# Weight loads of a two-layer encoder trunk: issued by Pool instead of SP

## The chip, the cores and the metric

One core of one Trainium2 chip. The core has five engines with queues of their own: TensorE (PE), VectorE (DVE), ScalarE (ACT), GpSimd (POOL) and SyncE (SP), and 16 DMA engines that they share. The metric is the device time of one execution in microseconds.

## The reference

Two encoder layers on 1024 tokens of width 1024, all in float32. In each layer

```
h = x * (1 + scale1(c)) + shift1(c)
x = LayerNorm(alpha * x + (1 + gate1(c)) * mix(h @ w_in) @ w_out)
h = x * (1 + scale2(c)) + shift2(c)
x = LayerNorm(alpha * x + (1 + gate2(c)) * (silu(h @ w_g) * (h @ w_u)) @ w_down)
```

`mix` is three groups of attention heads (A: differential, B: dilated windows, C: a local window with shared keys) side by side; `w_in` holds the queries, keys and values of all three. `w_g` and `w_u` stand side by side in `w_gu` (1024 x 5632, so 22 tiles of 128 columns each), `w_down` is 2816 x 1024. `scale`, `shift` and `gate` come from `silu(c) @ w_ada`.

## The kernel before

Activations lie transposed: a tile has 128 features on the partitions and tokens along the row. Every float32 product is made of three matmuls in a reduced format: each operand is split into a high part (ACT, a cast, line 162) and a low part (DVE, a subtraction, line 163), and high x high, high x low and low x high are summed (lines 302, 304, 306).

**Weights.** `load_w` (line 279) brings a column of 128 weights: for every four blocks of 128 rows one DMA (line 286) into a tile `raw` of 128 x 512 (256 KB, in runs of 512 bytes; 128 KB where only two blocks are left), which is then split into `wh` and `wl`. There are three `raw` buffers, two of `wh` and two of `wl`, so a load can start as soon as the split of the third load before it is done, and a split when PE has finished with the weights two columns back. `load_w` serves `w_in`, `w_out`, the first four tiles of the gate and `w_down`; for the very last group of `w_down` the split goes into 16 buffers `HW`, and all 8 columns are kept, as they are used twice.

**The gate.** Tiles 0 to 3 go through `gate` (line 1070) in two halves of the tokens with 32 loads by `load_w` in a layer. At the same time POOL makes the second half of the layer norm (lines 350, 372, 400) and the sums of the activations (`sums_h`, lines 1098 and 1101). The other 18 tiles go through `gate_all` (line 1111), a scheme with seven instead of eight block products: two DMAs of 512 KB (line 1120) fetch both columns into `E` (three buffers), POOL makes four sums of blocks `S1` to `S4` (line 1136), which are split into `WG` (10 buffers), PE makes the seven products (lines 1156 to 1158), POOL the last product with the silu (line 1195), and a DMA stores it (line 1196).

**Order.** Instructions are put in order on each engine by the framework's scheduler, which simulates a timeline; only some stretches of PE are kept in the order in which they are written. Each engine then works through its own row in order, and an instruction that waits holds up all that stand behind it on that engine. In the kernel before all DMAs are issued by SP: 1186 of them, of which the lines 286 and 1120 make 348 and 72. The rest are loads of `w_ada` (line 250), stores and fetches of attention's tiles (lines 570, 734 and others), of the hidden tiles (lines 1196, 1272) and of the output. POOL issues none; it rescales attention's probabilities (lines 597, 599, 881, 1019), and makes the parts of norm and gate named above.

Of the kernel before, what the change touches and what calls it, by code (L numbers as in the profile page):

```python
# [21 lines left out]
P = 128  # L22
NCH = 8
FH = 2816
# [80 lines left out]
class Trunk:  # L105
# [173 lines left out]
    def load_w(self, src, kt, parts=None):  # L279

        nc = self.nc
        wh, wl = parts or (self.t("wh", dt=F32R), self.t("wl", dt=F32R))
        for k in range(0, kt, 4):
            n = min(4, kt - k)
            raw = self.t("raw", (P, 512))
            nc.sync.dma_start(raw[:, :n * P].rearrange("p (k m) -> p k m", m=P), src[k * P:(k + n) * P].rearrange("(k p) m -> p k m", p=P))
            with self.tc.high_priority():
                self.split(wh[:, k * P:(k + n) * P], wl[:, k * P:(k + n) * P], raw[:, :n * P])
        return [a[:, :kt * P].rearrange("p (k m) -> p k m", m=P) for a in (wh, wl)]
# [120 lines left out]
    def first(self, X, H, side):  # L410
# [62 lines left out]

        columns(0, mods(0))
        wn = load_w(0)
        out = [self.t(tag, (P, 512)) for tag in ("S", "S", "S", "S", "MM", "MM")]
        for k in range(NCH):
            if k + 1 < NCH:
                acc = mods(k + 1)
            raw = wn  # L480
            if k + 1 < NCH:
                wn = load_w(k + 1)
            if k in self.X1:
                n = 4 // len(self.X1)
                for i in range(n):
                    load(4 + n * self.X1.index(k) + i)
            prepare(0, k)
            wh, wl = self.t("wh", dt=F32R), self.t("wl", dt=F32R)
            self.split(wh[:, :768], wl[:, :768], raw)
            ah, al = parts(H[k], 0)  # L490
            for c in range(6):
                w = slice(c * P, c * P + P)
                nc.tensor.matmul(out[c], wh[:, w], ah, start=k == 0, stop=False)
                nc.tensor.matmul(out[c], wh[:, w], al, start=False, stop=False)
                nc.tensor.matmul(out[c], wl[:, w], ah, start=False, stop=k == NCH - 1)
            if k + 1 < NCH:
                columns(k + 1, acc)
            for i in self.H1.get(k, ()):
                prepare(1, i)
            next(side, None)  # L500
# [610 lines left out]
    def gate_all(self, l, f, H, TS, hidden, last, side):  # L1111


        nc = self.nc
        q = [slice(256 * i, 256 * i + 256) for i in range(4)]
        raw = []
        for part in range(2):
            r = self.t("E")
            raw.append(r)
            nc.sync.dma_start(r.rearrange("p (k m) -> p k m", m=P), self.w_gu[l][:, part * FH + f * P:part * FH + (f + 1) * P].rearrange("(k p) m -> p k m", p=P))  # L1120
        a11, a12, a21, a22 = (raw[i // 2][:, 512 * (i % 2):512 * (i % 2) + 512] for i in range(4))
        ah, al = self.t("wh", dt=F32R), self.t("wl", dt=F32R)
        W = {}

        def ops(name, src):
            hi, lo = self.t("WG", (P, 512), F32R), self.t("WG", (P, 512), F32R)
            self.split(hi, lo, src)
            W[name] = (hi, lo)

        with self.tc.high_priority():  # L1130
            self.split(ah, al, raw[0])
            W["A11"], W["A12"] = ((ah[:, x], al[:, x]) for x in (slice(0, 512), slice(512, 1024)))
            s = {}
            for name, x, y, op in (("S1", a21, a22, ALU.add), ("S2", "S1", a11, ALU.subtract), ("S3", a11, a21, ALU.subtract), ("S4", a12, "S2", ALU.subtract)):
                s[name] = self.t("raw", (P, 512))
                nc.gpsimd.tensor_tensor(out=s[name], in0=s.get(x, x) if isinstance(x, str) else x, in1=s.get(y, y) if isinstance(y, str) else y, op=op)
                ops(name, s[name])
            ops("A22", a22)

        def quarter(name, half, j):  # L1140
            if name[0] == "T":
                c = q[int(name[1]) - 1]
                return [x[:, c] for x in TS[half, j]]
            k = 4 * (name[1] == "2") + j
            c = slice(256, 512) if name[2] == "1" else slice(0, 256)
            return [x[:, c] for x in H[k][half]]

        def product(tag, w, t):
            ps = self.t(tag, (P, 512))
            wh, wl = W[w]  # L1150
            for half in range(2):
                o = ps[:, 256 * half:256 * half + 256]
                for j in range(4):
                    c = slice(j * P, j * P + P)
                    th, tl = quarter(t, half, j)
                    nc.tensor.matmul(o, wh[:, c], th, start=j == 0, stop=False)  # L1156
                    nc.tensor.matmul(o, wh[:, c], tl, start=False, stop=False)  # L1157
                    nc.tensor.matmul(o, wl[:, c], th, start=False, stop=j == 3)  # L1158
            return ps

        prods = dict(P1=("MM", "A11", "B11"), P2=("MM", "A12", "B21"), P3=("TA", "S4", "B22"), P4=("S", "A22", "T4"),
                     P5=("S", "S1", "T1"), P6=("S", "S2", "T2"), P7=("S", "S3", "T3"))
        out = hidden[f].rearrange("p (h s c) -> p h s c", h=2, s=2)
        t = {}
        p = {}
        tt = lambda o, a, b, op: nc.vector.tensor_tensor(out=o, in0=a, in1=b, op=op)  # L1166
        new = lambda tag: self.t(tag, (P, 512))

        def step(n):
            p[n] = product(*prods[n])  # L1170
            next(side, None)

        def after1():
            t["a"] = new("ST")
            nc.scalar.copy(t["a"], p["P1"])

        def after6():
            t["b"] = new("ST")
            tt(t["b"], p["P6"], t["a"], ALU.add)

        def after7():
            t["c"] = new("TG")
            tt(t["c"], p["P7"], t["b"], ALU.add)

        def after5():
            t["d"] = new("TG")
            tt(t["d"], p["P5"], t["c"], ALU.add)
            tt(t["b"], p["P5"], t["b"], ALU.add)

        def after4():  # L1190
            tt(t["c"], t["c"], p["P4"], ALU.subtract)

        def finish(g, u, side):
            nc.scalar.activation(g, g, AF.Silu)  # L1194
            nc.gpsimd.tensor_tensor(out=u, in0=u, in1=g, op=ALU.mult)  # L1195
            nc.sync.dma_start(out[:, :, side], u.rearrange("p (h c) -> p h c", h=2))

        if last:
            for n in ("P6", "P7", "P5", "P4", "P1"):
                step(n)  # L1200
            after1(), after6(), after7(), after5(), after4()
        else:
            step("P1"), after1(), step("P6"), after6(), step("P7"), after7(), step("P5"), after5(), step("P4"), after4()
        step("P2")
        tt(t["a"], p["P2"], t["a"], ALU.add)
        finish(t["a"], t["c"], 1)
        step("P3")
        tt(t["b"], p["P3"], t["b"], ALU.add)
        finish(t["b"], t["d"], 0)
# [267 lines left out]
```

## Time and profile before

| | us |
|---|---|
| median of 3 runs | 2752.64 (2747.83 to 2754.9) |
| profiled execution | 2749.68 |
| its span, first to last instruction | 2747.8 |
| PE busy | 2603.6 (95%) |
| DVE busy | 1789.1 (65%) |
| ACT busy | 1122.0 (41%) |
| POOL busy | 866.7 (32%) |
| DMA engines, mean share | 40.0%, 332.90 MB, one queue of hardware |

The mean granted clock of TensorE was 0.982. The busy time of an engine counts neither its waits nor its issues of DMAs; SP's issues show as rows of `SPq` in the views of lines and queues. The stages of layer 1 lie, in us from the start of the span: norm and attention from 1398, `w_out` about 1930 to 2017, the first four tiles of the gate 2017 to 2125, `gate_all` 2125 to 2456, the down projection to 2683 and the last of it with the output to 2748. Layer 0 has the same stages from 50, 575, 664, 770 and 1130 on.

### The profile page before, as it was taken

To read this page: it belongs to the slowest core of one execution; us is meant where nothing else is said; L and a number is where in the kernel's file an instruction comes from. 1 tells how busy PE (TensorE), PEld (TensorE's weight loads), DVE (VectorE), ACT (ScalarE), POOL (GpSimd) and SP (SyncE) were. 2 spreads that over 40 slices of the span, in tenths; PEclk is the share of its full clock that TensorE was granted. 3 is DMA by queue.
4 is the path that set the end of the run, shared out by engine and by line. 5 is a ranking of instruction groups with operands and counts; after the bars stand their busy time and mean duration, and the time that the engine had idled before them with its cause. 6 is when DMAs were issued, how large, how long until landed. Compare 5 with 4: busy or idle time off the path is not lost.

```text
span 2747.8 us, 43777 instructions
## 1 busy us (share of the span) xinstructions
PE 2603.6 (95%) x16327; PEld 2217.1 (81%) x16327; DVE 1789.1 (65%) x3321; ACT 1122.0 (41%) x2255; POOL 866.7 (32%) x849
## 2 busy tenths in 40 slices
PE   6899988889999999999988999999999999999997
PEld 5788765668789999988867887766777999998887
DVE  7588746657867877745585887366487555545457
ACT  3466545523532222312244666466254323222124
POOL 4132322424634444200141323224256444430000
PEclk9999999999999999999999999999999999999999
DMA  8723342253454554643227223320425222236223
GB/s 270 223 79 92 128 125 75 56 184 89 158 157 146 169 154 143 195 161 105 74 88 236 81 77 119 107 57 10 138 89 180 89 77 86 78 100 215 81 81 115
DMA packets 389652, 335.69 MB, mean 122 GB/s; under 512 B 35096, under 2 KB 332096, under 8 KB 389440
## 3 DMA queue, kind: packets, MB, share of 16 engines
q1 hardware_dynamic: 389440, 332.90, 40.0%
q8 instruction: 129, 2.11, 0.3%
q14 instruction: 83, 0.68, 0.1%
HBM read 265.52 MB, written 67.31 MB: 121 GB/s over the span
## 4 chain that ended last, share of the span: by engine, by line
PE 60%; DMA 8%; DVE 7%; POOL 4%; issue 3%; ACT 2%; SPq 0%; DVEq 0%; POOLq 0%; ACTq 0%
PE S L306 5%; PE S L302 5%; PE S L304 5%; PE MM L306 4%; PE MM L302 4%; PE MM L304 4%; PE S L1156 4%; PE S L1157 4%; PE S L1158 4%; DMA MR<-in_w_ada 3%; PE MM L1158 2%; PE MM L1156 2%; PE MM L1157 2%; PE S L967 2%; PE MM L1042 1%
## 5 line engine op out<-in xcount | busy, mean ns | idle before, releaser
L162 ACT CAST wh<-raw 128x512 fp32r<-128x512 f32 x332 | 191.4, 603 | 518.1 <-PE S L304 224.7
L1156 PE MATMUL S<-O,WG 128*128 128x256 f32 x1152 | 325.1, 282 | 0.0
L1158 PE MATMUL S<-O,WG 128*128 128x256 f32 x1152 | 324.6, 282 | 0.0
L1157 PE MATMUL S<-O,WG 128*128 128x256 f32 x1152 | 324.4, 282 | 0.0
L163 DVE TENSOR_TENSOR wl<-raw,wh 128x512 fp32r<-128x512 f32 x332 | 259.7, 804 | 75.1 <-ACT wh L162 71.0
L306 PE MATMUL MM<-H,wl 128*128 128x512 f32 x624 | 248.9, 399 | 5.3 <-DVE wl L163 5.2
L302 PE MATMUL MM<-H,wh 128*128 128x512 f32 x624 | 247.8, 397 | 2.2 <-ACT wh L162 1.8
L304 PE MATMUL MM<-H,wh 128*128 128x512 f32 x624 | 249.0, 399 | 0.0
L1156 PEld LDWEIGHTS S<-O,WG 128*128 128x128 f32 x1152 | 217.1, 188 | 0.0
L1158 PEld LDWEIGHTS S<-O,WG 128*128 128x128 f32 x1152 | 217.0, 188 | 0.0
L1157 PEld LDWEIGHTS S<-O,WG 128*128 128x128 f32 x1152 | 217.0, 188 | 0.0
L162 ACT CAST WG<-raw 128x512 fp32r<-128x512 f32 x144 | 88.9, 621 | 289.0 <-PE S L1157 207.5
L1054 DVE SCALAR_TENSOR_TENSOR X<-S,der,X 128x512 f32<-128x512 f32 (+1 forms) x136 | 97.2, 718 | 162.4 <-PE S L306 150.8
L302 PE MATMUL S<-O,wh 128*128 128x512 f32 x496 | 193.4, 390 | 0.6 <-DVE der L274 0.6
L304 PE MATMUL S<-O,wh 128*128 128x512 f32 x496 | 193.0, 389 | 0.0
L306 PE MATMUL S<-O,wl 128*128 128x512 f32 x496 | 192.4, 391 | 0.5 <-DVE wl L163 0.5
L597 POOL TENSOR_SCALAR EX<-EX,Acf 128x384 f32<-128x384 f32 x64 | 70.2, 1098 | 386.8 <-DVE Acf L596 165.1
L1156 PE MATMUL MM<-H,wh 128*128 128x256 f32 x576 | 161.7, 281 | 1.1 <-DVE ST L1166 1.1
L1158 PE MATMUL MM<-H,wl 128*128 128x256 f32 x576 | 161.1, 280 | 0.9 <-DVE wl L163 0.9
L1157 PE MATMUL MM<-H,wh 128*128 128x256 f32 x576 | 161.0, 279 | 0.0
L1195 POOL TENSOR_TENSOR TG<-TG,ST 128x512 f32<-128x512 f32 x72 | 117.7, 1636 | 121.6 <-ACT ST L1194 69.3
L304 PEld LDWEIGHTS MM<-H,wh 128*128 128x128 f32 x624 | 118.5, 190 | 34.4 <-issue 8.4
(303 smaller groups left out, 6957.9 us busy)
## 6 DMA issues: line engine op xcount, KB each, us to landing
E<-in_w_gu SPq DMA_DIRECT2D x72, 512.0 KB, 4.4
MR<-in_w_ada SPq DMA_DIRECT2D x112, 256.0 KB, 3.0
raw<-in_w_down SPq DMA_DIRECT2D x96, 256.0 KB, 2.9
raw<-in_w_in SPq DMA_DIRECT2D x92, 256.0 KB, 3.9
E<-hid SPq DMA_DIRECT2D x44, 512.0 KB, 4.4
hid<-TG SPq DMA_DIRECT2D x72, 256.0 KB, 3.4
X<-ka SPq DMA_DIRECT2D x128, 128.0 KB, 4.1
raw<-in_w_out SPq DMA_DIRECT2D x64, 256.0 KB, 2.9
```

The source lines that it names most:

```text
L162: self.nc.scalar.copy(hi, src)
L163: self.nc.vector.tensor_tensor(out=lo, in0=src, in1=hi.bitcast(F32), op=ALU.subtract)
L302: nc.tensor.matmul(ps, wh[:, k], ah, start=k == order[0], stop=False)
L304: nc.tensor.matmul(ps, wh[:, k], al, start=False, stop=False)
L306: nc.tensor.matmul(ps, wl[:, k], ah, start=False, stop=k == order[-1])
L597: nc.gpsimd.tensor_scalar(out=e[1][:, 640:], in0=e[1][:, 640:], scalar1=cf[:, 1:2], scalar2=1.0, op0=ALU.mult, op1=ALU.mult)
L967: nc.tensor.matmul(S[:, r, u, cs], a, b, start=True, stop=True)
L1054: self.nc.vector.scalar_tensor_tensor(out=X[d][:, sl], in0=ps, scalar=self.der[l][:, b * 8 + d:b * 8 + d + 1], in1=X[d][:, sl], op0=ALU.mu ...
L1156: nc.tensor.matmul(o, wh[:, c], th, start=j == 0, stop=False)
L1157: nc.tensor.matmul(o, wh[:, c], tl, start=False, stop=False)
L1158: nc.tensor.matmul(o, wl[:, c], th, start=False, stop=j == 3)
L1195: nc.gpsimd.tensor_tensor(out=u, in0=u, in1=g, op=ALU.mult)
```

## The change

The DMAs of lines 286 and 1120 are issued by POOL. What they move, their buffers and their splits stay. SP keeps 766 DMAs.

```diff
@@ load_w
             raw = self.t("raw", (P, 512))
-            nc.sync.dma_start(raw[:, :n * P].rearrange("p (k m) -> p k m", m=P), src[k * P:(k + n) * P].rearrange("(k p) m -> p k m", p=P))
+            nc.gpsimd.dma_start(raw[:, :n * P].rearrange("p (k m) -> p k m", m=P), src[k * P:(k + n) * P].rearrange("(k p) m -> p k m", p=P))
             with self.tc.high_priority():
                 self.split(wh[:, k * P:(k + n) * P], wl[:, k * P:(k + n) * P], raw[:, :n * P])
@@ gate_all
             r = self.t("E")
             raw.append(r)
-            nc.sync.dma_start(r.rearrange("p (k m) -> p k m", m=P), self.w_gu[l][:, part * FH + f * P:part * FH + (f + 1) * P].rearrange("(k p) m -> p k m", p=P))
+            nc.gpsimd.dma_start(r.rearrange("p (k m) -> p k m", m=P), self.w_gu[l][:, part * FH + f * P:part * FH + (f + 1) * P].rearrange("(k p) m -> p k m", p=P))
```

The scheduler places the loads among POOL's instructions. First place: POOL in layer 0 while the first four tiles of the gate begin (in the names, the number behind a tile tells buffers of one tag apart). In the kernel before its row reads:

```order
L350 TENSOR_TENSOR ST_6168<-ST_6168,X_5688 128x512
L400 TENSOR_SCALAR ST_6297<-X_5678,der_138,sh_1300_6293 128x512
L400 TENSOR_SCALAR ST_6303<-X_5680,der_138,sh_1300_6293 128x512
L400 TENSOR_SCALAR ST_6346<-X_5682,der_138,sh_1300_6293 128x512
L400 TENSOR_SCALAR ST_6352<-X_5684,der_138,sh_1300_6293 128x512
L400 TENSOR_SCALAR ST_6395<-X_5686,der_138,sh_1300_6293 128x512
L350 TENSOR_TENSOR ST_6168<-ST_6168,X_5690 128x512
L400 TENSOR_SCALAR ST_6401<-X_5688,der_138,sh_1300_6293 128x512
```

In the changed kernel, from the same instruction on:

```order
L350 TENSOR_TENSOR ST_6168<-ST_6168,X_5688 128x512
L286 DMA raw_6521<-in_w_gu 128x4x128
L286 DMA raw_6569<-in_w_gu 128x4x128
L400 TENSOR_SCALAR ST_6297<-X_5678,der_138,sh_1300_6293 128x512
L400 TENSOR_SCALAR ST_6303<-X_5680,der_138,sh_1300_6293 128x512
L400 TENSOR_SCALAR ST_6346<-X_5682,der_138,sh_1300_6293 128x512
L400 TENSOR_SCALAR ST_6352<-X_5684,der_138,sh_1300_6293 128x512
L350 TENSOR_TENSOR ST_6168<-ST_6168,X_5690 128x512
L286 DMA raw_6573<-in_w_gu 128x4x128
L286 DMA raw_6635<-in_w_gu 128x4x128
L400 TENSOR_SCALAR ST_6395<-X_5686,der_138,sh_1300_6293 128x512
L400 TENSOR_SCALAR ST_6401<-X_5688,der_138,sh_1300_6293 128x512
```

The norm's steps of lines 350 and 400 stand in the same order as before, with a load or two of `in_w_gu` after every one to four of them; before, these loads followed one another in SP's row. Each waits there for its `raw` buffer, with the norm's next steps behind it.

Second place: POOL in `gate_all` of layer 0, tiles 5 and 6. Before:

```order
L1136 TENSOR_TENSOR raw_7863<-E_7837,raw_7851 128x512
L1136 TENSOR_TENSOR raw_8100<-E_8094 128x512
L1136 TENSOR_TENSOR raw_8106<-raw_8100,E_8092 128x512
L1136 TENSOR_TENSOR raw_8112<-E_8092,E_8094 128x512
L1195 TENSOR_TENSOR TG_7711<-TG_7711,ST_7646 128x512
L1195 TENSOR_TENSOR TG_7741<-TG_7741,ST_7673 128x512
L1136 TENSOR_TENSOR raw_8118<-E_8092,raw_8106 128x512
```

In the changed kernel, from the same instruction on:

```order
L1136 TENSOR_TENSOR raw_7863<-E_7837,raw_7851 128x512
L1120 DMA E_8094<-in_w_gu 128x8x128
L1136 TENSOR_TENSOR raw_8100<-E_8094 128x512
L1136 TENSOR_TENSOR raw_8106<-raw_8100,E_8092 128x512
L1136 TENSOR_TENSOR raw_8112<-E_8092,E_8094 128x512
L1195 TENSOR_TENSOR TG_7711<-TG_7711,ST_7646 128x512
L1120 DMA E_8346<-in_w_gu 128x8x128
L1195 TENSOR_TENSOR TG_7741<-TG_7741,ST_7673 128x512
L1136 TENSOR_TENSOR raw_8118<-E_8092,raw_8106 128x512
L1120 DMA E_8348<-in_w_gu 128x8x128
```

The two loads of a tile stand now directly in front of and between the last steps of the tile before it, and the second of them directly in front of the first sum that reads it. In SP's row they stood among loads of `w_ada` and stores.

Third place: the end of the program, where SP issued the last loads of `in_w_down` one after the other and then the stores of the output. On POOL, in the changed kernel, the row ends so:

```order
L286 DMA raw_26272<-in_w_down 128x4x128
L286 DMA raw_26276<-in_w_down 128x2x128
L286 DMA raw_26282<-in_w_down 128x4x128
L286 DMA raw_26286<-in_w_down 128x2x128
L1346 TENSOR_TENSOR O_26720<-O_26720,HR_26206 128x1024
L1473 UNCONDITIONAL_BRANCH
```

Nothing but loads stands there between them; the last POOL operation (line 1346) comes behind them all.

## Rows read from the trace of the kernel before

**Rows 1.** The page's busy times: engine, us, share, instructions.

```profile
PE 2603.6 (95%) x16327; PEld 2217.1 (81%) x16327; DVE 1789.1 (65%) x3321; ACT 1122.0 (41%) x2255; POOL 866.7 (32%) x849
```

**Rows 2.** The page's costliest groups: busy us, mean ns | idle us before, releaser.

```profile
L162 ACT CAST wh<-raw 128x512 fp32r<-128x512 f32 x332 | 191.4, 603 | 518.1 <-PE S L304 224.7
...
L162 ACT CAST WG<-raw 128x512 fp32r<-128x512 f32 x144 | 88.9, 621 | 289.0 <-PE S L1157 207.5
...
L597 POOL TENSOR_SCALAR EX<-EX,Acf 128x384 f32<-128x384 f32 x64 | 70.2, 1098 | 386.8 <-DVE Acf L596 165.1
...
L1195 POOL TENSOR_TENSOR TG<-TG,ST 128x512 f32<-128x512 f32 x72 | 117.7, 1636 | 121.6 <-ACT ST L1194 69.3
```

**Rows 3.** Table by stretches: length; busy PE, PEld, DVE, ACT, POOL; granted clock; DMA.

```profile
664.00:770.00 106.00, 99.27 (x434) 79.14 (x433) 86.31 (x125) 53.73 (x87) 65.12 (x55) 0.98 0.51 160
1398.00:1500.00 102.00, 88.18 (x384) 70.20 (x383) 64.82 (x109) 49.82 (x88) 26.18 (x23) 0.95 0.67 202
2017.00:2125.00 108.00, 101.32 (x449) 80.92 (x448) 86.24 (x125) 55.82 (x91) 66.13 (x56) 1.00 0.47 148
2125.00:2456.00 331.00, 331.00 (x2801) 329.77 (x2800) 178.24 (x220) 101.21 (x154) 144.12 (x103) 1.00 0.28 82
2683.00:2748.00 65.00, 50.92 (x392) 48.27 (x390) 46.48 (x113) 27.25 (x65) 2.34 (x1) 0.91 0.35 116
```

**Rows 4.** Waits of PE, 664 to 770: us, times, longest.

```profile
PE TA L302 <- ACT wh L162: 3.0, 2, 2.7
PE MM L306 <- DVE wl L163: 2.6, 3, 1.3
PE MM L302 <- ACT wh L162: 0.9, 1, 0.9
```

**Rows 5.** Line 286: durations in ns, min/median/max; landing.

```profile
L286 SPq DMA_DIRECT2D raw<-in_w_gu x64: 367/368/922, 664.8 to 2117.8; - x64
...
DMA to landing us min/median/max: 2.1/3.0/9.8
```

**Rows 6.** Waits of SP's queue, whole span.

```profile
SPq L286 <- DVE wl L163: 675.5, 221, 33.8
```

**Rows 7.** Line 1120: durations in ns; landing.

```profile
L1120 SPq DMA_DIRECT2D E<-in_w_gu x72: 367/379/603, 756.1 to 2435.3; - x72
...
DMA to landing us min/median/max: 3.7/4.4/6.4
```

**Rows 8.** One line's instructions (400).

```profile
L400 POOL TENSOR_SCALAR ST<-X,der,sh x40: 762/771/3080, 670.9 to 2083.6; 128x512 f32<-128x512 f32 x40
```

**Rows 9.** DMA issues, 664 to 770: KB each, median us to landing.

```profile
raw<-in_w_gu SPq DMA_DIRECT2D x32, 256.0 KB, 3.2
```

**Rows 10.** Waits of SP's queue, 664 to 770.

```profile
SPq L286 <- DVE wl L163: 47.6, 20, 7.9
```

**Rows 11.** SP's queue in order of time, 2683 to 2712: start, us.

```profile
2682.70 24.64 SPq L286 DMA_DIRECT2D raw<-in_w_down  x17
```

**Rows 12.** DMA issues, 2683 to 2712.

```profile
raw<-in_w_down SPq DMA_DIRECT2D x8, 256.0 KB, 2.9
raw<-in_w_down SPq DMA_DIRECT2D x9, 128.0 KB, 2.5
```

**Rows 13.** Waits of ACT, 2683 to 2712.

```profile
ACT HW L162 <- DMA raw<-in_w_down: 13.0, 8, 2.9
```

**Rows 14.** Waits of POOL, 2150 to 2456.

```profile
POOL raw L1136 <- DMA E<-in_w_gu: 61.0, 15, 5.0
```

**Rows 15.** Waits of SP's queue, 1398 to 1500.

```profile
SPq L286 <- DVE wl L163: 29.8, 15, 6.8
```

**Rows 16.** Waits of PE, 1398 to 1500.

```profile
PE TA L530 <- ACT ST L527: 5.5, 1, 5.5
PE S L386 <- DVE rsy L319: 5.4, 1, 5.4
```

**Rows 17.** Groups of POOL, 664 to 770.

```profile
L1098 POOL TENSOR_SCALAR E<-X,der 128x512 f32<-128x512 f32 x16 | 25.1, 1579 | 7.4 <-DVE O L163 5.0 <-DVE E L1101 2.3
```

## Prediction, made before the changed kernel was run

> **What bounds the kernel now.** Five views were read, from the whole to the place where the change bites. First the busy time of each engine: PE works 2603.6 of a span of 2747.8 us [rows 1], so all that is not matmul is 144.2 us, and a change that touches no matmul can take at most that away, while it can add without limit. Second the costliest groups: the 332 casts into `wh` stood idle 518.1 us, most of it waiting for PE to let go of a buffer, and the 144 casts into `WG` 289.0 us for the same reason [rows 2]. Over most of the program the weights are therefore ahead of PE and wait for it. Third the table by stretches, to find where that isn't so: in 664 to 770 us and 2017 to 2125 us (the first four tiles of the gate in each layer) DVE is busy 86.3 of 106 and 86.2 of 108 us and POOL 65.1 and 66.1, while in 2125 to 2456 (`gate_all`) PE is busy all 331.0 us [rows 3]. Fourth the waits inside the first of these stretches: PE there waits for a `wh` cast or a `wl` subtraction, that is for weights, in 6.5 us altogether [rows 4]; short, but it says that a later weight is a later PE. Fifth the queue of SP: a 256 KB load holds SP for about 0.37 us and lands some 3 us later [rows 5]; SP itself waited 675.5 us for a free `raw` buffer [rows 6], which cost nothing, as little behind it was urgent. POOL has no DMA in this trace, so the price of an issue from POOL is the one number that must be bounded.
>
> **The price of an issue from POOL.** 348 loads of `raw` and 72 of `E` move. On SP the issue takes 0.37 us [rows 5, 7]; that is the low end. The high end is the whole time from issue to landing, 3.0 us for `raw` and 4.4 us for `E` [rows 5, 7]: what SP leaves to hardware can hardly keep POOL longer than the transfer lasts now. The nearest rows of POOL's own work are on tiles of the same 128x512: 1.64 us for the products of line 1195 [rows 2], 0.76 us for line 400 undisturbed, but up to 3.08 [rows 8]. I take 1.5 us for a load of 256 KB, between these, half of it for the 128 KB loads at the end, and 2.2 us for 512 KB.
>
> The Trainium skill bears on this on both sides. DMA: Bandwidth & Descriptors, section "SWDGE vs HWDGE vs iDMA", says that a DMA from GpSimd has its descriptors computed by software on that engine, one from SP by hardware; its "Anatomy of one DMA" calls this generation "small, variable" beside a fixed 2 us. By that the issue would lie near the low end and the sum near nothing. No run so far shows it; it is the second rival below.
>
> **Gate, first four tiles (twice).** In 664 to 770 us SP issues 32 loads of `in_w_gu` of 256 KB [rows 9]; the loads of `E`, from 756 us on [rows 7], can slide into the next stretch. Afterwards POOL has its 65.1 us of work and 32 x 1.5 = 48 us of issues: 113.1 us in a stretch of 106. It waited besides for DVE and ACT in this stretch, and SP's 20 waits for a free `raw` buffer here, 47.6 us [rows 10], now stand in POOL's row, in front of the layer norm's and the sums' instructions (lines 400, 1098, 1101): a blocked load holds up the H tiles and the sums, and a long POOL instruction holds up the next load. Most of these waits vanish because loads come later; I keep 6 us. So 119 us instead of 106, +13; in layer 1 66.1 + 48 + 6 = 120 instead of 108, +12. With three `raw` buffers, and PE already waiting for weights there [rows 4], that delay reaches PE nearly in full. At the low end, 0.37 us, 32 issues are 12 us and POOL 77 of 106 us: about nothing. At the high end 65 + 96 + 6 = 167: +61 and +60.
>
> **The last weights.** From 2682.70 us SP issues 17 loads in 24.64 us, 8 of 256 and 9 of 128 KB, and ACT waits 13.0 us for them [rows 11 to 13]: three buffers go round and the loads are the pace. POOL is nearly idle there (2.3 us, [rows 3]), so only the longer issue counts: 8 x 1.5 + 9 x 0.75 = 18.8 us on POOL, under the 24.6 us, so POOL doesn't become the bound, but 1.1 us more (0.4 for the small ones) in each turn of a loop of three: (8 x 1.1 + 9 x 0.4) / 3 = 4.1 us; with the queueing I take +5. Low end 0; high end 8 x 3.0 + 9 x 1.5 = 37.5, so +13.
>
> **gate_all.** The 18 tiles of a layer bring 36 loads of 512 KB between POOL's sums and products. POOL works 144.1 of 331 us [rows 3], and 36 x 2.2 = 79 us more make 223: there is room. A sum waits for its `E` load 15 times, 61.0 us in all [rows 14], so a later landing of 2 us shifts the sums; but the casts behind them wait for PE, not the reverse [rows 2]. Cost 0. If that cover were gone, 18 tiles x 2 layers x 1 us = 36 us. At the high end of 4.4 us it is 302 of 331 us, still within.
>
> **Attention, w_out, w_down.** The rescaling of line 597 stands in front of a POOL that was idle 386.8 us before 64 of them, 6.0 us each [rows 2]; two issues of 1.5 us fit into one such gap, and the loads there are taken far ahead of PE. Now and then a transposed block comes 1 us later: I take +3 over all (0 to 20). In the down projections POOL is all but empty and DVE and the casts wait for PE: 0.
>
> **What SP gains.** Without 420 loads, and without its 675.5 us of waits [rows 6], SP issues stores and fetches earlier. In 1398 to 1500 us loads wait for `raw` buffers on SP 29.8 us with stores and fetches behind them [rows 15], but PE waits there for the norm's rsqrt and a tile of ACT, 5.4 and 5.5 us [rows 16], not for a load or fetch. I take -3 (0 to -15).
>
> **Sum.** +13 +12 +5 +0 +3 -3 = +30 us on the profiled execution's 2749.7 us, which is 2779.7; the median of the runs shown lies 2.9 us above that execution, so 2782 us.
>
> **Rivals.**
> *The issue is short or covered.* At 0.4 to 0.7 us an issue, POOL in the tight stretches has 78 to 88 of 106 us to do and the other terms cancel: 2750 to 2756, say 2753. For it: PE waits only 6.5 us for weights there [rows 4]. Against: POOL's waits for DVE in between can't all be filled.
> *POOL's issue is stretched by DVE.* POOL's line 400 takes 0.76 us alone and up to 3.08 [rows 8], and in the tight stretch, where DVE is busiest, line 1098 on a tile of the same shape takes 1.58 on average [rows 17]. If an issue is stretched likewise, to 2.3 us, the tight stretches become 65 + 74 + 6 = 145 and 146 us (+39, +38), the end +8, the rest 0: +85, or 2838. At 3.0 us all through it is +61 +60 +13 = +134, or 2887. It decides from a mean issue of 2 us in these stretches on. The Trainium skill has such a rule: SBUF — State Buffer, "SBUF: two separate sides", says that GpSimd can't write descriptors while DVE holds the shared port pair in a two-port operation, and gives 620 ns alone against 3100 ns beside a copy. No run so far shows a DMA of POOL; POOL's stretched operations are the trace's own hint of it.
> *SP relieved: faster.* The place is the norm, attention and w_in of both layers, where PE's idle time is: 102 - 88.2 = 13.8 us in 1398 to 1500 [rows 3] alone. If a store or fetch of `ka`, `kv` or `X` behind a blocked load on SP is what ends some of these idle times, and the issue is under 0.7 us so that the tight stretches cost nothing, 10 us come back: 2743. Against it: the waits named there are for DVE and ACT [rows 16].
> That the change does not do what it says is excluded: the order of POOL's instructions shows the 420 loads, and PE has the same instructions.
>
> **How the numbers follow.** About 8 us (0.3%) is what a measurement here can tell from no change. Chances: forecast (2765 to 2800) 0.43, stretched issue 0.27, short issue 0.17, SP relieved 0.13. All of the first two is slower, 0.70; same 0.17; faster 0.13. The range takes in the short issue and half of the relief below and nearly all of the stretched issue above: 2744 to 2865.
>
> **What would show it.** In the profile of the changed kernel: POOL rows of DMA at lines 286 and 1120, with their duration (1.5 and 2.2 us by the forecast; under 0.7 the short issue; over 2 and wider in spread in 664 to 770 us the stretched one). The two gate stretches longer by some 12 us each, PE idle there on `ACT wh` and `DVE wl`, and POOL at over 95% of them. The last stage longer by 5 us with ACT waiting for `raw`. `gate_all` with PE still at 100%. I would be wrong if the loss sits in attention or in gate_all, or if PE's idle falls in 1398 to 1500 us.

## The result, and the profile after

The changed kernel takes 2785.97 us (median of 4 runs, 2779.91 to 2793.92), the kernel before 2753.77 in the runs beside it: a ratio of 1.0118 with a 95% interval of 1.0097 to 1.0140, so 32 us slower. The forecast was 2782. The sum came out; most of its terms didn't, and the experiments show that errors cancelled in it.

The page of the changed kernel, its busy times and its DMA queues (packets, MB, share of 16 engines), against [rows 1]:

```profile
PE 2618.2 (94%) x16327; PEld 2225.6 (80%) x16327; DVE 1787.8 (64%) x3321; ACT 1124.4 (40%) x2255; POOL 1175.6 (42%) x1269
...
q1 hardware_dynamic: 139008, 208.09, 23.8%
q0 software_dynamic: 37184, 124.81, 15.7%
```

The span is 2778.6 us. POOL is busy 309 us more. Its issues count as busy time on this engine: 316 x 0.75 + 32 x 0.70 + 72 x 0.93 = 326 us by the rows below; the rest of its work came out some 17 us shorter. PE's idle time grew from 144.2 to 160.4 us, that is by 16 us, and its busy time for the same instructions by 14.6: after a wait PE ran at the lower clock for a while (granted mean 0.977 instead of 0.982). So nearly half of the loss is not a wait, but what follows one.

Lines 286 and 1120, durations in ns and landing, against [rows 5, 7]; they are rows of POOL now:

```profile
L286 POOL DMA_DIRECT2D raw<-in_w_down x128: 702/747/807, 1153.1 to 2739.6; - x128
...
L286 POOL DMA_DIRECT2D raw<-in_w_gu x64: 747/770/804, 670.5 to 2147.9; - x64
...
DMA to landing us min/median/max: 2.5/3.5/11.0
```

```profile
L1120 POOL DMA_DIRECT2D E<-in_w_gu x72: 882/928/937, 771.3 to 2464.8; - x72
...
DMA to landing us min/median/max: 4.6/5.1/7.9
```

An issue takes POOL 0.75 us for 256 KB (forecast 1.5) and 0.93 for 512 KB (forecast 2.2). In the tight stretches, where DVE is busiest, it is the same: from 0.747 to 0.804 us.

The table by stretches, for the stretches of [rows 3] in the same order, moved by what PE had lost up to each:

```profile
671.00:778.00 107.00, 100.10 (x434) 78.70 (x433) 92.44 (x128) 53.81 (x87) 82.68 (x87) 0.98 0.46 147
1420.00:1525.00 105.00, 91.48 (x386) 72.57 (x385) 67.82 (x110) 49.25 (x88) 51.56 (x55) 0.93 0.66 195
...
2041.00:2154.00 113.00, 104.53 (x449) 82.73 (x448) 86.58 (x122) 55.32 (x89) 86.88 (x89) 0.97 0.43 137
2154.00:2485.00 331.00, 330.49 (x2797) 329.17 (x2796) 161.73 (x221) 102.29 (x156) 180.41 (x137) 1.00 0.27 83
2712.00:2778.60 66.60, 51.78 (x393) 48.42 (x391) 46.83 (x113) 27.98 (x65) 14.75 (x18) 0.91 0.34 113
```

The first tight stretch is 1 us longer, the second 5; `gate_all` of layer 1 loses nothing. In the first the loads do come late for ACT, which waited 5.8 us for them before, but PE waits no longer than before (6.8 us, [rows 4] 6.5), and most of it for the norm's H tile:

```profile
ACT wh L162 <- DMA raw<-in_w_gu: 23.3, 13, 3.9
```

```profile
PE MM L304 <- DVE H L163: 4.4, 3, 2.8
PE MM L306 <- DVE wl L163: 1.3, 1, 1.3
PE TA L306 <- DVE wl L163: 1.1, 2, 0.7
```

To see where the 31 us went, the start of the same count of matmuls on PE is compared in both traces; the entries are us lost in each stretch, by the times of the kernel before (the experiments' kernels stand there already, from one profiled execution each; stretches with the same work differ by some 3 us, in 400 to 664 by more, and the sum is that of the one execution, which for `only_raw` lies 6 us below the median of its runs and for `stores_later_sp` 9 above).

| kernel | 0-400 | 400-664 | gate 0, first four, 664-788 | gate_all 0, 788-1145 | 1145-1500 | 1500-1930 | w_out 1, 1930-2017 | gate 1, first four, 2017-2128 | 2128-2683 | end | sum |
|---|---|---|---|---|---|---|---|---|---|---|---|
| changed | 7.3 | 0.0 | 1.9 | 11.5 | 4.3 | 1.0 | -2.9 | 5.1 | 0.9 | 1.5 | 30.8 |
| order_after_sp | 3.7 | -3.0 | -1.0 | 7.5 | -4.3 | -0.1 | 1.0 | -0.6 | 0.0 | 0.4 | 3.6 |
| order_before_pool | 0.6 | 3.1 | 8.5 | 11.9 | 0.8 | -1.1 | -4.5 | 10.2 | 0.5 | 3.6 | 33.6 |
| only_raw | 5.3 | -3.2 | -1.3 | -0.1 | 2.0 | 1.3 | -4.5 | 5.2 | 2.5 | 0.8 | 8.1 |
| only_E | 0.0 | -0.3 | 0.5 | 15.7 | -1.3 | -2.0 | 0.7 | 0.5 | 0.7 | 0.0 | 14.5 |
| stores_later_sp | -1.9 | 7.5 | 3.6 | 10.5 | 2.0 | -1.9 | 0.0 | 1.9 | 0.0 | 0.0 | 21.8 |
| stores_later_E | 0.4 | 5.3 | 1.8 | -2.5 | 6.3 | -3.2 | -1.5 | 0.0 | 0.7 | 0.0 | 7.1 |
| load_after_product | -0.5 | -0.8 | 2.1 | 10.8 | 4.1 | -0.9 | -1.6 | 0.3 | 0.8 | 0.2 | 14.4 |
| pool_time_only (0.33 us) | 1.0 | 5.3 | 0.9 | 6.2 | -2.6 | -1.9 | -1.6 | 3.4 | 3.2 | 1.0 | 14.7 |
| pool_time_full (0.69 us) | 2.4 | 4.8 | 5.0 | 1.6 | -2.4 | -0.5 | 0.0 | 6.3 | 3.2 | 0.7 | 21.1 |
| two_issues | 2.3 | 10.8 | 23.8 | 9.9 | 6.9 | -1.4 | -1.9 | 22.6 | 0.8 | 4.8 | 78.5 |
| gate_first_four | 1.1 | 1.1 | 7.5 | 3.2 | 1.0 | -1.9 | 0.1 | 8.1 | 0.0 | 1.1 | 21.3 |
| w_out_layer1 | 0.9 | -1.1 | 1.8 | 3.1 | 0.9 | -1.5 | -4.5 | 1.3 | 0.0 | 1.0 | 1.8 |

### The profile page after: what moved, and what is told of

Read it like the earlier page. It is cut to its first block, busy times and chain, and to the rows that moved or that the text cites. A ratio compares the mean times of both kernels' runs of the same rounds, so it can differ in the third digit from the quotient of the medians.

```text
span 2778.6 us, 43862 instructions
## 1 busy us (share of the span) xinstructions
PE 2618.2 (94%) x16327; PEld 2225.6 (80%) x16327; DVE 1787.8 (64%) x3321; ACT 1124.4 (40%) x2255; POOL 1175.6 (42%) x1269
## 3 DMA queue, kind: packets, MB, share of 16 engines
q1 hardware_dynamic: 139008, 208.09, 23.8%
q0 software_dynamic: 37184, 124.81, 15.7%
## 5 line engine op out<-in xcount | busy, mean ns | idle before, releaser
L286 POOL DMA_DIRECT2D raw<-in_w_down x128 | 95.2, 745 | 379.8 <-DVE wl L163 354.3
```

The source lines that it names most:

```text
L286: nc.gpsimd.dma_start(raw[:, :n * P].rearrange("p (k m) -> p k m", m=P), src[k * P:(k + n) * P].rearrange("(k p) m -> p k m", p=P))
```

## The experiments

**Order or issue?** In `gate_all` of layer 0 PE waits in its row for DVE at line 268, whose place the scheduler had moved, and near 110 us a `wl` stands behind another DVE instruction than before. So a first theory was that the new order costs the time, not POOL. The order of each engine can be held: after the program is traced, its instructions are chained without semaphores in a given order (the tables hold numbers of instructions as the other kernel's scheduler had put them; the moved loads are left out of them, so the scheduler places these).

```diff
     with tile.TileContext(nc, schedule_with_timeline_sim=True) as tc:
         trunk(tc, *args)
+        fix_order(tc)
...
+def fix_order(tc):
...
+            if last is not None:
+                tc.add_manual_dep(i, last, dep, reason='order')
+            last = i.name
```

`order_after_sp`: the kernel before with the changed kernel's order.

> Loads issued by SP as before, but the instructions of PE, DVE, ACT, the computing ones of POOL and the other DMAs of SP are chained in the order that the scheduler gave the changed kernel. Theory of the order (the loss comes from where the scheduler, which simulates a timeline, put the other engines' instructions once the loads were POOL's): as slow as the changed kernel, about 2780 to 2790 us, with PE waiting at line 268 in gate_all of layer 0 and for wl near 110 us. Theory of the issue (0.75 us of POOL's time per load and the queue behind it): back to 2750 to 2757 us.

`order_before_pool`: the changed kernel with the order of before.

> The mirror image: loads issued by POOL, all other instructions chained in the order of the kernel before. Theory of the order: 2750 to 2757 us, though POOL spends 0.75 us on each load. Theory of the issue: 2780 to 2790 us. If both have a share, the two kernels' losses should add up to about 31 us.

Measured: 1.0013 (0.9998 to 1.0027) and 1.0120 (1.0100 to 1.0141). As the cause of the whole loss the order has fallen: alone it is worth some 4 us (0 to 7 by the interval), the issue from POOL in the old order all of the loss. But the order decides where the loss shows: with the order of before, the first four gate tiles lose 8.5 and 10.2 us; with the scheduler's new order they lose 6.6 and 5.1 less, and other stretches lose more. With all loads on SP the new order loses 7.5 us in `gate_all` of layer 0 in its one profile, and wins as much back elsewhere; so the changed kernel's 11.5 us there need not all be the issue's. (POOL's own steps changed places too: in the first excerpt of the change, line 400 on `X_5686` stands behind line 350 on `X_5690`, before it stood in front of it.)

In the kernel with the order of before the forecast's mechanism is to be seen (stretch table, then the largest wait of ACT and all waits of PE in the first tight stretch):

```profile
668.00:781.00 113.00, 102.13 (x430) 80.55 (x429) 88.19 (x124) 53.46 (x87) 83.92 (x89) 0.95 0.48 148
2037.00:2155.00 118.00, 106.11 (x448) 83.28 (x447) 84.90 (x121) 55.98 (x91) 87.09 (x90) 0.96 0.43 136
```

```profile
ACT wh L162 <- DMA raw<-in_w_gu: 18.8, 7, 5.0
```

```profile
PE MM L306 <- DVE wl L163: 4.6, 3, 1.9
PE TA L302 <- ACT wh L162: 3.9, 3, 2.7
PE MM L302 <- ACT wh L162: 2.2, 2, 1.7
```

PE has 10.7 us of waits there instead of the 6.5 of [rows 4], and 2.9 us more of busy time at a granted clock of 0.95 instead of 0.98. POOL is at 84 of 113 us, far from full, and yet the loads come late.

**Which loads?**

```diff
 # only_raw: line 286 as changed, line 1120 stays
-            nc.gpsimd.dma_start(r.rearrange("p (k m) -> p k m", m=P), ...
+            nc.sync.dma_start(r.rearrange("p (k m) -> p k m", m=P), ...
 # only_E: line 1120 as changed, line 286 stays
-            nc.gpsimd.dma_start(raw[:, :n * P].rearrange("p (k m) -> p k m", m=P), ...
+            nc.sync.dma_start(raw[:, :n * P].rearrange("p (k m) -> p k m", m=P), ...
```

> Only line 286 (348 loads of raw) on POOL, line 1120 on SP. The order of PE is near that of the changed kernel (118 lines of difference). By the stretches in which the changed kernel fell behind: if gate_all's 12 us come from its own loads (line 1120), 2768 to 2775 us; if they come from the order of DVE and SP around the loads of w_ada, which is kept nearly whole here, 2778 to 2788 us.

> Only line 1120 (72 loads of E) on POOL; PE and ACT keep the order of the kernel before exactly. Theory of the issue in gate_all: +10 to +15 us, 2763 to 2768. Theory of the order: within 4 us of the kernel before, 2750 to 2757 us.

Measured: `only_raw` 1.0047 (1.0027 to 1.0067), 13 us, 2763.5; `only_E` 1.0067 (1.0043 to 1.0091), 18 us, 2767.1. Together they make 31 of the 32. `only_raw` came out below both of its expectations, `only_E` as the theory of the issue had it. The 72 loads of `E`, for which the forecast had nothing, cost about as much as the 348 of `raw` (the intervals overlap), and in the profile all of it is in `gate_all` of layer 0; in that of layer 1, where the same loads stand between the same sums and products, it is 0.7 us. What layer 0 has besides is the w_ada of the next layer, fetched by SP (line 250) and added up by DVE in its own row (line 254).

In both kernels the scheduler chose the order. In `only_E` PE and ACT keep theirs, but in `gate_all` of layer 0 DVE's additions of line 254 moved forward in its row near 885, 990 and 1074 us, close to where PE loses time, so the 15.7 us of that stretch are issue and order together. In `order_before_pool` and in `load_after_product` below, where DVE keeps the order of before, it loses 11.9 and 10.8 us.

**The first four gate tiles alone.**

```diff
-            w = self.load_w(self.w_gu[l][:, part * FH + f * P:part * FH + (f + 1) * P], NCH)
+            w = self.load_w(self.w_gu[l][:, part * FH + f * P:part * FH + (f + 1) * P], NCH, None, nc.gpsimd)
```

(`load_w` takes the issuing engine as a further argument, SP without it; the order of before is held.)

> Only the 64 loads of in_w_gu by line 286 (first four gate tiles of both layers) on POOL, all else on SP, the order of the kernel before. It measures the forecast's main term alone. By the forecast's step (POOL full at 1.5 us an issue) with the measured 0.75 us POOL would have 65 + 24 = 89 of 106 us to do and the term would be near nothing: 2750 to 2756 us. If the late load is the cause, the stretches lose 8 and 10 us as they do in the kernel with all loads on POOL: 2768 to 2774 us.

Measured: 1.0056 (1.0037 to 1.0074), 15.5 us, in the range of the late load; the profile has 7.5 and 8.1 us in these two stretches, and in the first ACT waits 16.0 us for `raw` with POOL busy for 81 of 112 us. So this term exists without POOL being full.

**POOL's time, or the load's place in POOL's row?** In these two SP issues everything as before, and POOL spends the time of an issue at the place where the load stood. A load then never waits for POOL, nor POOL for a buffer.

```diff
+    def spend(self):
+        for i in range(8):
+            self.nc.gpsimd.memset(self.idle[:, i:i + 1], 0.0)
...
+            self.spend()
             nc.sync.dma_start(raw[:, :n * P]...
```

> All loads issued by SP in the order of the kernel before; in front of the place that each of the 420 loads had in POOL's row stand eight small memsets (about 0.1 us each), so POOL loses the time of an issue, but no load waits for POOL. Theory of POOL's time (norm, sums and products come later): most of the 32 us, 2772 to 2790 us. Theory of the late load (a load stands behind POOL's work and is issued too late): 2750 to 2760 us, with a loss in gate_all of layer 0 at most.

Eight memsets took 0.33 us together, not 0.75; measured 1.0040 (1.0022 to 1.0057), 2766.2 us, between the two ranges. With nineteen:

> As the kernel with eight memsets before each load's place, but nineteen, since eight took only 0.33 us: POOL now loses 0.78 us for each of the 420 loads, about an issue's time, and SP issues all loads in the order of before. Theory of POOL's time: 2775 to 2790 us, like the loads on POOL. Theory of the late load: the tight gate stretches lose under half of their 18 us, gate_all of layer 0 all of its 12: 2764 to 2774 us.

Nineteen took 0.69 us, a little under an issue. Measured: 1.0051 (1.0034 to 1.0068), 14 us, in the range of the late load, but not with the parts that it named. In the first four gate tiles 5.0 and 6.3 us, where the loads on POOL lost 8.5 and 10.2: by these single executions some 60% is norm and sums that come later. The rest, by the difference, is the late load or POOL's own wait for a buffer; these kernels leave out both at once. In `gate_all` of layer 0 it is 1.6 us instead of 11.9 (though 6.2 with half the time, so single executions scatter there): POOL's time doesn't account for that loss.

**A dearer issue.** Each load of 256 KB is made by two DMAs of 128 KB; the order of before is held.

```diff
-            nc.gpsimd.dma_start(raw[:, :n * P]..., src[k * P:(k + n) * P]...)
+            for j in range(0, n, 2):
+                nc.gpsimd.dma_start(raw[:, j * P:(j + 2) * P]..., src[(k + j) * P:(k + j + 2) * P]...)
```

> All loads on POOL, other instructions in the order of the kernel before; each load of 256 KB is made by two DMAs of 128 KB, so a tile of raw costs POOL about 2 x 0.70 = 1.40 us instead of 0.75, near the 1.5 us that the forecast assumed. By the forecast's sum with 1.5 us for raw and the measured rest: the first four gate tiles +12 to +25 us in each layer, the end +5, gate_all +13: 2790 to 2815 us. If the late load grows with the issue, as each waits behind the one before, rather 2815 to 2840 us.

Measured: 1.0262 (1.0231 to 1.0293), 72 us, 2826.9, in the range of the late load that grows with the issue, at 0.72 us for each half:

```profile
L287 POOL DMA_DIRECT2D raw<-in_w_gu x128: 702/720/759, 679.1 to 2194.0; - x128
```

This is nearly the price that the forecast took, 1.44 us for a tile of `raw`, though made by twice as many DMAs, which the forecast didn't have. The first four gate tiles then lose 23.8 and 22.6 us, not 13 and 12. So the forecast's sum was right at half the price and, as far as this kernel stands for a dearer issue, would have been wrong by 40 us at its own.

**gate_all of layer 0.** Waits there in the kernel before, then in the changed one: of PE for DVE to empty a bank, of SP for a product, and of DVE for w_ada (us, times, longest).

```profile
PE MM L268 <- DVE ST L1166: 1.4, 2, 1.1
```

```profile
SPq L1196 <- POOL TG L1195: 80.8, 24, 10.9
```

```profile
DVE MA L254 <- DMA MR<-in_w_ada: 58.7, 36, 7.5
```

```profile
PE MM L268 <- DVE ST L1166: 6.8, 3, 3.6
```

```profile
SPq L1196 <- POOL TG L1195: 123.6, 29, 19.9
```

```profile
DVE MA L254 <- DMA MR<-in_w_ada: 70.5, 42, 9.2
```

The chain that this suggests: SP stands longer at the stores, the loads of w_ada stand behind them, DVE waits for these in its row with the sums that empty PE's banks behind, and PE waits for the bank. To cut it, each store is put up to three loads of w_ada later in SP's row, once with all loads on SP (control) and once with line 1120 on POOL.

```order
L250 DMA MR_8024<-in_w_ada 128x512
L250 DMA MR_8053<-in_w_ada 128x512
L1196 DMA hid_5_6497<-TG_7711 256x1x256
L250 DMA MR_8085<-in_w_ada 128x512
L250 DMA MR_8153<-in_w_ada 128x512
L250 DMA MR_8183<-in_w_ada 128x512
L1196 DMA hid_5_6497<-TG_7741 256x1x256
```

(SP's row in `stores_later_E`; without the shift the first of these stores stands in front of `MR_8024`, the second in front of `MR_8085`.)

> All loads issued by SP and all instructions in the order of the kernel before, except that in gate_all every store of line 1196 stands up to three loads of w_ada later in SP's row. It is the control of the next kernel. Both theories: within 6 us of the kernel before, 2744 to 2756 us; a gain is possible, since the loads of w_ada wait behind stores in the kernel before as well (DVE waits 60.5 us for them there).

> Only line 1120 on POOL, the order of the kernel before, with the same shift of the stores. Theory of the chain (POOL's issue delays the product of line 1195, SP's store waits for it, the loads of w_ada stand behind the store, DVE waits for them in its row and PE for DVE): most of the 18 us goes, 2748 to 2757 us. Rival (the E loads land 0.7 us later and the sums with them, whatever SP does): still 2762 to 2770 us.

Measured: the control 1.0038 (1.0023 to 1.0052), outside its expectation: the shift alone costs 10 us; with line 1120 on POOL 1.0022 (1.0006 to 1.0038), 2761.1 us, between its two ranges. So with the stores later, moving the `E` loads to POOL costs nothing more (4 us less than the control, where the intervals overlap) instead of 18; together the two still cost 6 us. In the profile with line 1120 on POOL `gate_all` of layer 0 takes 2.5 us less than before, and DVE waits

```profile
DVE MA L254 <- DMA MR<-in_w_ada: 54.1, 39, 6.8
```

The control speaks against the first link of the chain. SP waits less for products there than in the kernel before, and yet DVE waits longer for w_ada and the stretch loses 10.5 us:

```profile
SPq L1196 <- POOL TG L1195: 63.8, 16, 11.2
```

```profile
DVE MA L254 <- DMA MR<-in_w_ada: 74.9, 39, 7.8
```

Another link was to be the load in front of the second product: in POOL's row 29 loads were put behind it instead (order of before held, only line 1120 on POOL).

```diff
 # POOL's row in gate_all
 L1195 product
-L1120 load
 L1195 product
+L1120 load
 L1136 sum
```

> Only line 1120 on POOL and the order of the kernel before, but in POOL's row of gate_all 29 loads that stood between the two products of line 1195 stand behind the second. Theory of the chain (a load that waits for its E buffer holds up the second product, SP's store waits for it, and behind the store the loads of w_ada for which DVE waits): well under half of the 18 us that the kernel with line 1120 alone on POOL lost, 2750 to 2762 us, and SP waits 80 to 95 us for products in gate_all of layer 0 instead of 121. Rival (it is the second load in front of the sums, or the later landing): 2764 to 2772 us.

Measured: 1.0070 (1.0055 to 1.0084), 2767.7 us, in the rival's range and no better than `only_E`; SP waits 108.5 us for products (120.8 in `only_E`, 80 to 95 expected), DVE 76.5 for w_ada. The load between the products is not the cause. What stays, by one execution of each kernel: the stretch loses about 10 us or more only where DVE waits 68 us or more for w_ada, whatever SP waits for products, and PE's waits there are for DVE. The place of the stores in SP's row moves the loss by 10 us and more, up with the `E` loads on SP and down with them on POOL. So the loss is in the meeting of stores, w_ada loads and DVE's row. What makes w_ada late is open: the `E` loads' later landing (5.1 instead of 4.4 us), the moments at which they now meet w_ada's transfers, or SP's row without their waits.

**A part that gains.** With `w_out` of layer 1 on POOL, `order_before_pool` and `only_raw` run through 1930 to 2017 us 4.5 us faster, the changed kernel 2.9 and `two_issues` 1.9. PE in the kernel before, there (start, us, line; idle before it in brackets):

```profile
1956.14 0.50 PE L302 MATMUL MM<-O,wh 128*128 128x512 f32 x1 [2.17 <-ACT wh L162]
...
1958.42 0.63 PE L304 MATMUL MM<-O,wh 128*128 128x512 f32 x1
1958.85 0.63 PE L306 MATMUL MM<-O,wl 128*128 128x512 f32 x1
```

PE waits 2.17 us for weights. Soon after, from 1957.5 to 1961 us, it runs at the lower of its two clocks (granted 0.51, against 1.00 from 1940 to 1953 us): a matmul starts 0.43 us after the one before instead of 0.23. The 13 matmuls up to 1961 us take 5.1 us here and 2.9 in `w_out_layer1` below, where this wait is gone; the lower clock costs as much again as the wait. On SP these loads were issued behind eight fetches of X, and the first of them landed some 10 us later, after the fetches. Only they are moved:

```diff
-                    wt = self.load_w(self.w_out[l][:, d * P:(d + 1) * P], NCH)
+                    wt = self.load_w(self.w_out[l][:, d * P:(d + 1) * P], NCH, None, (self.nc.sync, self.nc.gpsimd)[l])
```

> Only the 32 loads of w_out of layer 1 on POOL, all else on SP, the order of the kernel before. On SP these loads stand behind seven fetches of X that wait for PE, and PE waits 2.2 us for them and then runs 2 us at the lower clock; on POOL they don't. If this gain of 4.5 us is SP's relief and costs nothing elsewhere: 2746 to 2750 us, faster than both kernels. If it was only the later course of the program before it: 2751 to 2756 us.

Measured: 0.9994 (0.9983 to 1.0005), 2754.1 us, in the second range. The 4.5 us are in its profile, and PE's wait for `wh` is gone there, but the whole run can't be told from the kernel before. No gain is shown.

## Why the prediction was right, and where it was not

- *The price of an issue.* Taken as 1.5 and 2.2 us by POOL's operations of the same shape; measured 0.75 and 0.93. The bounds held, the choice between them didn't: an issue isn't an operation on 128x512 elements. It depends little on the size (0.70, 0.75, 0.93 us for 128, 256, 512 KB).
- *Gate, first four tiles, +13 and +12.* Place and direction are right: moved alone they lose 15.5 us. In the changed kernel 1.9 and 5.1 are left, as the scheduler gave other engines another order. POOL's wait for buffers in the first, taken as 6 us, is 6.0 in the changed kernel. The step that failed is the reasoning by POOL's busy time: at 0.75 us it gives 65 + 24 = 89 of 106 us and no loss, and at 1.44 us half of the measured loss. POOL's row need not be full (77% busy in the changed kernel, not the 95% that was to show it). A load waits for the instruction in front of it, an H tile or a sum for the load, and a late weight or H tile costs PE a wait and then some time at the lower clock.
- *The last weights, +5:* 1.5 in the changed kernel, 3.6 in the order of before, 4.8 at 0.72 us for each half. At the measured price the same sum gives (8 x 0.38 + 9 x 0.33) / 3 = 2.0. That fits a right mechanism and a price too large, but single executions scatter by as much.
- *gate_all, 0:* wrong in layer 0 (+11.5), right in layer 1 (+0.8). By the prediction's own sign ("wrong if the loss sits in attention or in gate_all") this is where its mechanism failed. "The casts behind them wait for PE" was true of the casts; the step overlooked that in layer 0 DVE waits 58.7 us for w_ada in its own row, and that SP's row, from which the loads were taken, holds the stores and w_ada. The cover that was named belonged to another engine than the one that came late.
- *Attention, +3:* 3.1 us in 125 to 400 and 1.7 in 1500 to 1720, but with the new order and all loads on SP 125 to 400 loses 3.9 as well. The size agrees; that it comes from the loads isn't shown.
- *What SP gains, -3:* 2.9 us, but in `w_out` of layer 1 and not in 1398 to 1500, where the changed kernel lost 2.7 us.
- *Not foreseen:* 4.2 us up to 125 us. There a DVE cast that waits 8.8 us for a table now stands in front of the `wl` for which PE waits 6.0 us. With the order of before this loss is gone; with the new order and all loads on SP it is gone too, as the cast then waits 6.0 us and PE 0.2. It takes both, the order and the issue. Nor was a loss of 5.5 us from 1145 to 1200 us foreseen, most of which 1320 to 1398 wins back; its cause is open.
- *The rival of the stretched issue.* It is refuted by the rows: from 0.747 to 0.804 us in the tight stretches, with DVE busy 92 of 107 us in the first. A rule of the Trainium skill (SBUF — State Buffer, "SBUF: two separate sides") speaks of DVE operations that hold the shared port pair, as copies in a two-port mode do; no run here shows such a lock on an issue, nor whether DVE ran such an operation beside one. The Trainium skill (DMA: Bandwidth & Descriptors, "Anatomy of one DMA") calls the generation of the descriptors small and variable. The whole issue takes 0.70 to 0.93 us here; how much of that is the generation, no run shows.
- *The rival of the short issue* (the first in the prediction's list, not the second) nearly had the price (0.4 to 0.7 us, measured 0.75) and would have missed the time by 33 us.

So that the time came out is in good part luck: the price was twice too high, the loss per us of issue in the first four gate tiles too low by about as much (in the order of before), and in the changed kernel 11 us came from a stretch that had been put at nothing.

## What to carry to other kernels

What an issue costs on a compute engine isn't its duration against that engine's free time, but what stands behind it in that row and behind the rows that it leaves: look through the row of every engine of the chain, not only of the one that takes the load. In a stage where PE already waits for weights, loads that come later by an instruction of the new issuer can cost, whatever the average says: here the new issuer was busy for 81 of 112 us. And before a loss is explained by new waits at new places, hold the order and move only the issuer: here the places of the loss changed with the order, and the sum hardly did. What one stretch lost in one execution is weak evidence; whole runs, repeated, decide.

## What the runs showed of the hardware that was not expected

- POOL's issue takes nearly the same time for the three sizes: 0.70 us for 128 KB (256 runs of 512 bytes), 0.75 for 256 KB, 0.93 for 512 KB; SP's took 0.37 to 0.38 for all. Two halves cost twice 0.72.
- DMAs from POOL show as another queue with larger packets: 37184 packets for 124.81 MB, 3.4 KB each; on SP the same bytes were 250432 packets of about 0.5 KB (389440 before less 139008 left). They don't land sooner for it: 3.5 instead of 3.0 us and 5.1 instead of 4.4.
- A wait of 2.2 us of PE was followed by 3.5 us at a granted clock of 0.51, in which a matmul started every 0.43 instead of 0.23 us; 13 matmuls took 2.1 us longer, so this short wait cost about double. Over the changed kernel PE's waits grew by 16 us and its busy time by 15.
- Small POOL memsets of 128x1 that follow one another cost about 0.04 us each, though each shows as 0.098 us.
